# A hybrid diffusion step on one core: attention's exponentials added ahead of their sums, and GpSimd's passes given to other engines

## Chip, core and metric

The kernel runs on one core of a Trainium2 chip. The core has TensorE (PE, matmuls into PSUM), VectorE (DVE), ScalarE (ACT), GpSimd (POOL) and SyncE (SP, which issues nearly all transfers). The metric is the device time of one execution in microseconds (us).

## What is computed

Two layers work on 1152 tokens of 1024 values: 1024 latent tokens and 128 prompt tokens. Each layer normalises and modulates x, projects it once into columns for three groups of heads, and projects their joined output back. Cut to what matters (the prompt attends to itself alone, the latent tokens to 128 cached keys as well):

```python
def trunk_layer(x, cvec, l, P, ctx=None):
    shift, scale, gate = adaln(cvec, P['w_mod'][l], P['b_mod'][l])
    u = layer_norm(x) * (1.0 + scale) + shift
    r, k, v, g, cq, ckv, kr, gm, xl, gl = split_in(u @ P['w_in'][l])
    ...
    y_rw, S_fin = rwkv_branch(u, r, k, v, g, S0, l, P)            # a scan over tokens, both ways
    y_mla = block_attention(qn, qr, kn, kr_all, vv) * jax.nn.silu(gm)
    y_lru, h_fin = lru_branch(xl, gl, h0, l, P)
    out = jnp.concatenate([y_rw, y_mla, y_lru], axis=-1) @ P['w_out'][l]
    return layer_norm(ALPHA * x + gate * out, P['ln_g'][l], P['ln_b'][l]), ...

def one_block(args):                                              # of block_attention
    s = (jnp.einsum('bqhd,bkhd->bhqk', qn_b, kn) + jnp.einsum('bqhr,bkr->bhqk', qr_b, kr)) * SOFTMAX_SCALE
    p = jax.nn.softmax(s, axis=-1)
    return jnp.einsum('bhqk,bkhd->bqhd', p, v)
```

## The kernel before

All matrices are float32. A product of full precision is made from a rounded high part and a low part that is the difference (`mm3`: three products); the "splits" of the text make these parts, the high one by a copy that rounds (DVE or ACT), the low one by a subtraction.

A layer runs in four stages. (1) Tokens, nine tiles of 128 in a fixed order: `load_x`, `norm_x` (statistics, POOL's power for the root, normalisation), `norm_u` (transposes on PE, shift and scale on ACT), `make_u` (high and low part), a matmul of 288 columns for v and the rope key, and the rotation of that key by six small DVE passes, a transpose and a DMA. (2) Features, groups of columns over all tokens, with the conv, gates and scans of the LRU (`lru_piece`) and the queries between them; the modulation of what comes later is computed here in pieces (`adaln_piece`, a generator with two halves: matmul and copy, then a small matmul that reads the copy). (3) Slots, 48 in a layer: 8 heads times 2 halves of the queries are 16 units of attention, and each takes 3 slots of 3 blocks of 128 keys. (4) The output projection with the last LayerNorm, tile by tile; in layer 0 the first two tiles of layer 1 are normalised in it.

The slots are written out by hand. Each has six blocks (A0, G, A1, B, C, S), filled through `at(slot, block, f)`; in a slot, the engines take the instructions in that order, as `line` keeps it. The slot loop (L1335 on) runs A0, the scores and exponentials of three blocks of keys, G, A1, B, the values, C, the sums and S. Between the attention lie the maxima of the queries to come (`max_q`, `max_last`, DVE's reduce over 1024 columns of the one PSUM buffer "b"), the scan (`win_*`: products for a tile of tokens; `inv_*`: the inverse of 64x64 blocks, by 15 pairs of POOL instructions on growing shapes; `chain_*`: the scan itself, PE with DVE copies in blocks C and B), and the group norm and gates of the outputs. `vtt`, `vts` and `vstt` are DVE's tensor-tensor, tensor-scalar and scalar-tensor-tensor forms, `gtt` is POOL's tensor-tensor, `act` and `sca_` are ACT. In the profile most of them bear the line of a helper (L116; matmuls L121); those of POOL bear their own. The sums over keys are those of the slot:

```python
for j, pe in u["pe"]:                   # three blocks of 128 keys x 512 queries
    for qt in range(4):
        mm(u["sum"][32 * qt:32 * qt + 32, 0:128], lhsT=two[:, 0:32], rhs=pe[:, 128 * qt:128 * qt + 128], ...)
```

A float32 matmul is issued as two PE instructions. Outside the slots a planner of the framework orders the work. The kernel's start loads x of two tiles, then the modulation's weights of layer 0 in eight pieces (`adaln_all`), then the first weights of the tokens.

## Time and profile before

| | us |
|---|---|
| median of 3 runs (1920.42 to 1930.34) | 1920.56 |
| the profiled execution, its whole time | 1929.06 |
| its span, first to last instruction | 1927.3 |
| PE busy | 1802.6 (94%) |
| DVE busy | 1177.3 (61%) |
| ACT busy | 944.1 (49%) |
| POOL busy | 588.9 (31%) |

The mean granted clock of PE is 0.969 of full speed. The rows below are of four kinds. A row of busy times has the stretch in us from the start of the span, its length, then the busy time (and number of instructions) of PE, PE's weight loads, DVE, ACT and POOL, the granted clock, the share of time in which the DMA engines were busy, and GB/s. A row of a timeline has the start, the duration, engine, line, operation, the names out<-in, the shapes, and how many are joined in the row; in brackets the idle time before it and who ended that. A row of groups has the busy time of all, the mean in ns of one, the idle time before and its releasers. A row of waits has the sum, the number and the longest.

### The profile page before, as it was taken

The page shows a single profiled execution, that of the slowest core. Times are in us where ns is not written, and L with a number is a line of the kernel's source. Part 1 is how long each engine was busy: PE and PEld are TensorE (multiplying, and loading weights), DVE is VectorE, ACT ScalarE, POOL GpSimd, SP SyncE. Part 2 cuts the span into 40 slices and gives each one's busy share as a digit, 9 for nine tenths or more (in the row PEclk, how much of TensorE's full clock was granted, in tenths as well). Part 3 has the DMA queues.
Part 4 walks back from the last instruction along what each step waited for, and adds up shares of the span by engine and source line. Part 5 has one row for each costly group of instructions (what it writes and reads, how often), then busy time and mean ns, then how long its engine had stood idle before and what let it go on. Part 6 is the DMA issues. An engine that isn't in the chain of part 4 may idle for free.

```text
span 1927.3 us, 47961 instructions
## 1 busy us (share of the span) xinstructions
PE 1802.6 (94%) x18782; PEld 1510.9 (78%) x18782; DVE 1177.3 (61%) x2454; ACT 944.1 (49%) x2159; POOL 588.9 (31%) x1055
## 2 busy tenths in 40 slices
PE   6899999889999999998978999999889999999897
PEld 4798888877787777766867999998767777777586
DVE  6744444784555655765778353548755566666576
ACT  2542556773444544554225335678544454555421
POOL 1411002032344434322645110111235344342253
PEclk8999999989999999999988999999899999999899
DMA  8335444674344444436443252435633433333642
GB/s 303 100 98 166 122 131 134 213 233 126 76 113 109 112 109 108 120 104 200 153 141 115 85 185 78 133 103 193 202 93 77 99 91 86 84 86 86 214 131 88
DMA packets 329091, 250.39 MB, mean 130 GB/s; under 512 B 105304, under 2 KB 268704, under 8 KB 327840
## 3 DMA queue, kind: packets, MB, share of 16 engines
q1 hardware_dynamic: 328864, 247.32, 43.7%
q8 instruction: 148, 2.42, 0.5%
q14 instruction: 79, 0.65, 0.1%
HBM read 168.55 MB, written 78.64 MB: 128 GB/s over the span
## 4 chain that ended last, share of the span: by engine, by line
PE 56%; DVE 7%; DMA 6%; ACT 4%; issue 3%; POOL 1%; SPq 1%; DVEq 0%; POOLq 0%; ACTq 0%
PE ps_a L121 36%; PE ps_pv L121 7%; PE ps_b L121 5%; PE ps_cx L121 4%; PE ps_rw L121 4%; DVE rw L116 2%; DVE sm L116 2%; DVE ls L116 1%; DVE t L116 1%; ACT rw L116 1%; ACT t L116 1%; DMA mxb<-inv_d 1%; ACT pe L116 1%; POOL rw L1416 1%; DMA kp<-in_wout_dram 1%
## 5 line engine op out<-in xcount | busy, mean ns | idle before, releaser
L121 PE MATMUL ps_a<-t,t 128*128 128x384 f32 (+4 forms) x6096 | 710.5, 295 | 20.7 <-DVE t L116 7.5
L121 PEld LDWEIGHTS ps_a<-t,t 128*128 128x128 f32 (+1 forms) x6096 | 652.9, 167 | 50.0 <-ACT pe L116 12.3
L116 DVE TENSOR_REDUCE sm<-ps_b 128x1 f32<-128x1024 f32 (+1 forms) x164 | 179.8, 1096 | 124.6 <-PE ps_b L121 124.2
L116 ACT ACTIVATE pe<-ps_a 128x512 f32<-128x512 f32 (+1 forms) x296 | 168.6, 576 | 175.0 <-PE ps_a L121 163.2
L121 PE MATMUL ps_a<-q,t 128*128 128x512 f32 x864 | 221.3, 401 | 4.9 <-DVE ep L116 4.9
L121 PEld LDWEIGHTS ps_a<-q,t 128*128 128x128 f32 x864 | 161.2, 190 | 47.9 <-issue 7.5
L121 PE MATMUL ps_a<-t,q 128*128 128x512 f32 (+1 forms) x544 | 163.5, 384 | 0.0
L116 DVE TENSOR_TENSOR t<-kp,t 128x512 fp32r<-128x512 f32 (+2 forms) x128 | 87.4, 710 | 106.5 <-ACT t L116 106.4
L121 PE MATMUL ps_pv<-pe,t 128*64 128x256 f32 x928 | 124.3, 389 | 0.0
L121 PEld LDWEIGHTS ps_a<-t,q 128*128 128x128 f32 x544 | 101.0, 190 | 22.2
L121 PE MATMUL ps_a<-t,kp 128*128 128x512 f32 (+1 forms) x304 | 118.0, 388 | 0.0
L116 ACT CAST t<-kp 128x512 fp32r<-128x512 f32 (+2 forms) x128 | 72.1, 600 | 84.8 <-DMA kp<-in_wft_dram 39.6
L121 PE MATMUL ps_b<-t,q 96*128 96x512 f32 (+1 forms) x384 | 107.3, 374 | 2.6 <-ACT t L116 1.5
L524 POOL TENSOR_TENSOR rw<-rw 128x512 f32<-128x512 f32 (+1 forms) x24 | 19.9, 831 | 262.6 <-ACT rw L116 174.5
L861 POOL TENSOR_TENSOR t<-t 64x15 f32<-64x15 f32 (+2 forms) x270 | 71.9, 266 | 58.9 <-DVE t L116 22.0
L121 PEld LDWEIGHTS ps_pv<-pe,t 128*64 128x64 f32 x928 | 59.7, 137 | 34.2 <-issue 7.7
L116 ACT ACTIVATE rw<-rw,sm 128x512 f32<-128x512 f32 x35 | 26.7, 809 | 119.6 <-DVE sm L116 115.9
L157 POOL TENSOR_TENSOR sm<-sm,nhalf 128x1 f32<-128x1 f32 (+1 forms) x54 | 34.1, 632 | 162.4 <-DVE sm L116 159.7
L121 PEld LDWEIGHTS ps_b<-t,q 96*128 96x128 f32 x384 | 61.9, 190 | 25.3 <-issue 9.9
L862 POOL TENSOR_TENSOR t<-t 64x15 f32<-64x15 f32 (+2 forms) x270 | 73.0, 270 | 20.4
L116 DVE TENSOR_TENSOR t<-ps_a,t 128x512 f32<-128x512 f32 (+2 forms) x106 | 65.5, 625 | 17.4 <-ACT t L116 9.7
L121 PE MATMUL ps_rw<-pe,two 128*32 128x128 f32 x1888 | 75.5, 277 | 0.0
(262 smaller groups left out, 3154.9 us busy)
## 6 DMA issues: line engine op xcount, KB each, us to landing
kp<-in_wft_dram SPq DMA_DIRECT2D x64, 256.0 KB
...
t<-v_d SPq DMA_DIRECT2D x144, 64.0 KB
```

The lines of the kernel that those rows point to most:

```text
L116: return lambda *a, **k: in_line(getattr(self.eng, op)(*a, **k))
L121: return in_line(nc.tensor.matmul(*a, **k))
L157: gtt(out, t[:, :n], nhalf.to_broadcast([128, n]), op=POW)
L524: gtt(q_, a_, a_, op=MUL)
L861: gtt(tv, U_[0:64, 0:t, t:t + 1].to_broadcast([64, t, n]), X[0:64, t:t + 1, t:16].to_broadcast([64, t, n]), op=MUL)
L862: gtt(X[0:64, 0:t, t:16], X[0:64, 0:t, t:16], tv, op=ADD)
L1416: (vtt if end and j else gtt)(z, z, lgb[:, 0, js], op=MUL)
```

## The change

The diff does six things.

1. Sums: DVE adds the exponentials of a slot's three blocks (`add_exps`, after A1 and after C), and `sums` takes one block instead of three, one slot later and ahead of the values. The reciprocal (`invert`) and what follows it move one slot back.
2. POOL's tensor passes become DVE's: the low split of u and of q, the sum of the rope queries, the square in the LRU, the gates, the masks of the window, the blocks of the inverse, two passes of the group norm, the low split and a product in the output projection. POOL keeps the powers, memsets and the pairs of `inv_blocks16`, which are now taken one by one through sixteen blocks of the order.
3. `norm_x` normalises on ACT; of four modulations in `norm_u` DVE makes one; the last LayerNorm is two DVE passes a half instead of ACT, POOL and DVE.
4. The rope keys stay in one tile, and `rope_tiles` rotates all of them in the loop of stage 2 that makes the queries' and keys' rows, at its third tile.
5. Start: the vectors of both layers are loaded and worked on first; the modulation's pieces come in the order 0, 4, 1, 5, then the first token weights, then 2, 6, 3, 7; the 1 of 1 + scale is added with the bias.
6. In the features the second half of a modulation piece runs with the next step (`ada_steps`) instead of at once.

Its changed lines, with the heads of functions (lines of context are left out; "..." stands between the hunks):

```diff
     def ada_mod(ada, pm, m0, nj):
-        vtt(modT[:, m0:m0 + nj, :], pm[:, 0:2 * nj].rearrange("p (j s) -> p j s", s=2),
-            vec[:, V_BM + m0:V_BM + m0 + nj, None].to_broadcast([128, nj, 2]), op=ADD)
-    def ada_one(modT):
-        vec_.tensor_scalar(modT[:, 8:16, :], modT[:, 8:16, :], 1.0, None, op0=ADD)
+        vstt(modT[:, m0:m0 + nj, :], pm[:, 0:2 * nj].rearrange("p (j s) -> p j s", s=2), 1.0 if m0 >= 8 else 0.0,
+             vec[:, V_BM + m0:V_BM + m0 + nj, None].to_broadcast([128, nj, 2]), ADD, ADD)
     def ada_mm(ps, cw, wm):
...
-    def adaln_all(l, ada):
-        for n in range(8):
+    def adaln_all(l, ada, ns):
+        for n in ns:
-            pm = P("rw")
+            pm = P("pv")
-        ada_one(ada[1])
     def adaln_piece(l, ada, n, half_):
...
-            if (n, half_) == (7, 1):
-                ada_one(ada[1])
...
+        vstt(mv[:, 3:4], mv[:, 0:1], -1.0, mv[:, 2:3], MUL, MUL)
-            vts(xt, xt, mv[:, 0:1], mv[:, 2:3], op0=SUB, op1=MUL)
+            act(xt, xt, AF.Identity, bias=mv[:, 3:4], scale=mv[:, 2:3])
     def norm_u(l, modT, i, tag="rw2"):
...
-                act(uf[:, j, :], ps[:, 128 * j:128 * j + 128], AF.Identity, bias=modT[:, k, s:s + 1], scale=modT[:, 8 + k, s:s + 1])
+                pj, sc, sh = ps[:, 128 * j:128 * j + 128], modT[:, 8 + k, s:s + 1], modT[:, k, s:s + 1]
+                if j < 3:
+                    act(uf[:, j, :], pj, AF.Identity, bias=sh, scale=sc)
+                else:
+                    vts(uf[:, j, :], pj, sc, sh, op0=MUL, op1=ADD)
-    ada = adaln_begin(0)
-    adaln_all(0, ada)
-    w1 = first_weights(0)
-    for l in range(layers):
-        last = l == L - 1
-        vec, modT, gate_row = ada
-        def vc(base, i=0, n=1):
-            return vec[:, base + i:base + i + n]
+    def layer_vectors(l, vec):
...
+        return hv, kah, omk, m4sp
+    adas = [adaln_begin(l_) for l_ in range(layers)]
+    lvec = [layer_vectors(l_, adas[l_][0]) for l_ in range(layers)]
+    ada = adas[0]
+    adaln_all(0, ada, (0, 4, 1, 5))
+    w1 = first_weights(0)
+    adaln_all(0, ada, (2, 6, 3, 7))
+    for l in range(layers):
+        last = l == L - 1
+        vec, modT, gate_row = ada
+        def vc(base, i=0, n=1):
+            return vec[:, base + i:base + i + n]
+        hv, kah, omk, m4sp = lvec[l]
...
-                gtt(Ub[b][1][:, 4 * hf:4 * hf + 4, cs], uf, hi, op=SUB)
+                vtt(Ub[b][1][:, 4 * hf:4 * hf + 4, cs], uf, hi, op=SUB)
...
+        kr = W("ls", [128, NTILE, 16, 2])
...
-            vt = W("pe", [128, 288])
-            sca_.copy(vt, ps[:, :288])
-            dma(v_d[ts_].rearrange("t e f c -> t (e f c)"), vt[:, 0:256])
-            kr = vt[:, 256:288]
+            vt = W("pe", [128, 256])
+            sca_.copy(vt, ps[:, :256])
+            dma(v_d[ts_].rearrange("t e f c -> t (e f c)"), vt)
+            vec_.tensor_copy(kr[:, i].rearrange("p j e -> p (j e)"), ps[:, 256:288])
-                dma(kr_out[l], kr)
-            kx = kr.rearrange("p (j e) -> p j e", e=2)
-            tr = W("ls", [128, 6, 16])
-            ko = W("ep", [128, 2, 16])
-            vtt(tr[:, 0], kx[:, :, 0], kcos[:, i], op=MUL)
-            vtt(tr[:, 1], kx[:, :, 1], ksin[:, i], op=MUL)
-            vtt(tr[:, 2], kx[:, :, 0], ksin[:, i], op=MUL)
-            vtt(tr[:, 3], kx[:, :, 1], kcos[:, i], op=MUL)
-            vtt(ko[:, 0], tr[:, 0], tr[:, 1], op=SUB)
-            vtt(ko[:, 1], tr[:, 2], tr[:, 3], op=ADD)
-            pt = P("pv" if n_ % 2 else "b")
-            transpose(pt[:32, :128], ko.rearrange("p a b -> p (a b)"), ident)
-            kT = W("ls", [32, 128])
-            sca_.copy(kT, pt[:32, :128])
-            dma(krT_d[:, 128 + 128 * i:256 + 128 * i], kT)
+                dma(kr_out[l], kr[:, i].rearrange("p j e -> p (j e)"))
+        def rope_tiles():
+            tr, ko = W("pe", [128, 3, NTILE, 16]), W("ls", [128, NTILE, 2, 16])
+            vtt(tr[:, 0], kr[:, :, :, 0], kcos, op=MUL)
+            vtt(tr[:, 1], kr[:, :, :, 1], ksin, op=MUL)
+            vtt(ko[:, :, 0], tr[:, 0], tr[:, 1], op=SUB)
+            vtt(tr[:, 2], kr[:, :, :, 0], ksin, op=MUL)
+            vtt(tr[:, 0], kr[:, :, :, 1], kcos, op=MUL)
+            vtt(ko[:, :, 1], tr[:, 2], tr[:, 0], op=ADD)
+            pt = P("pv")
+            for b in range(3):
+                transpose(pt[:96, 128 * b:128 * b + 128], ko[:, 3 * b:3 * b + 3].rearrange("p i a j -> p (i a j)"), ident)
+            kT = W("pe", [96, 3, 128])
+            sca_.copy(kT, pt[:96, :384].rearrange("p (b t) -> p b t", b=3))
+            for q_ in range(3):
+                dma(krT_d[:, 128:128 + NT].rearrange("c (b i t) -> i c b t", b=3, i=3)[q_], kT[32 * q_:32 * q_ + 32])
...
-                gtt(t1, t1, t2, op=ADD)
+                vtt(t1, t1, t2, op=ADD)
...
+            if i == 2:
+                rope_tiles()
...
-                gtt(q_, a_, a_, op=MUL)
+                vtt(q_, a_, a_, op=MUL)
...
-            ada = adaln_begin(l + 1)
+            ada = adas[l + 1]
+        ada_open = []
+        def ada_steps():
+            for piece in ada_open:
+                next(piece, None)
+            ada_open.clear()
...
+            ada_steps()
-                for _ in adaln_piece(*todo):
-                    pass
+                ada_open.append(adaln_piece(*todo))
+                next(ada_open[-1])
...
-                    gtt(v_, v_, mask[:, d, None, 64:128].to_broadcast([128, 4, 64]), op=MUL)
+                    vtt(v_, v_, mask[:, d, None, 64:128].to_broadcast([128, 4, 64]), op=MUL)
         def win_transposes(i):
...
+                yield
...
-                gtt(Of[:, d].rearrange("p a (b c) -> p a b c", b=4), abz[:, d].rearrange("p f s (b c) -> p (f s) b c", b=4),
+                vtt(Of[:, d].rearrange("p a (b c) -> p a b c", b=4), abz[:, d].rearrange("p f s (b c) -> p (f s) b c", b=4),
         def inv_blocks():
-            for o, t_, ttt in ((1, BdT, vtt), (0, Bd, gtt)):
-                ttt(t_.rearrange("p d a (b j) -> p (d a) b j", b=4), Bdc[:, o, :, None, :].to_broadcast([128, 8, 4, 16]),
+            for o, t_ in ((1, BdT), (0, Bd)):
+                vtt(t_.rearrange("p d a (b j) -> p (d a) b j", b=4), Bdc[:, o, :, None, :].to_broadcast([128, 8, 4, 16]),
         def inv_product(i, n):
...
-            gtt(y4, y4, lnx[:, 1, None].to_broadcast([128, n, 2, 64]), op=ADD)
+            vtt(y4, y4, lnx[:, 1, None].to_broadcast([128, n, 2, 64]), op=ADD)
-            gtt(vt8, vt8, bon[:, c0:c0 + n].rearrange("p c f -> p (c f)")[:, :, None].to_broadcast([128, g, 64]), op=MUL)
+            vtt(vt8, vt8, bon[:, c0:c0 + n].rearrange("p c f -> p (c f)")[:, :, None].to_broadcast([128, g, 64]), op=MUL)
...
-            gtt(qo[0:96], ql, qh[0:96], op=SUB)
+        def split_low(u):
+            qo = u["qo"]
+            vtt(qo[0:96], qo[0:96].bitcast(F32), u["qh"][0:96], op=SUB)
         def max_q(u, qt):
...
-        def sums(u):
+        def sums(u, pe, first, last_):
-            for j, pe in u["pe"]:
-                if j == 0:
-                    u["sum"] = P("rw")
-                for qt in range(4):
-                    mm(u["sum"][32 * qt:32 * qt + 32, 0:128], lhsT=two[:, 0:32], rhs=pe[:, 128 * qt:128 * qt + 128],
-                       start=j == 0, stop=j == end)
-                if j == end:
-                    u["rl"] = W("ls", [128, 128])
-                    vec_.reciprocal(u["rl"], u["sum"][:, 0:128])
-            u["pe"] = []
+            if first == 0:
+                u["sum"] = P("rw")
+            for qt in range(4):
+                mm(u["sum"][32 * qt:32 * qt + 32, 0:128], lhsT=two[:, 0:32], rhs=pe[:, 128 * qt:128 * qt + 128],
+                   start=first == 0, stop=last_ == end)
+        def invert(u):
+            u["rl"] = w2[:, u["i"] % 2, 0:128]
+            vec_.reciprocal(u["rl"], u["sum"][:, 0:128])
+        def add_exps(u, n):
+            if n == 1:
+                u["acc"] = W("ls", [128, 512])
+                vtt(u["acc"], u["pe"][0][1], u["pe"][1][1], op=ADD)
+            else:
+                vtt(u["acc"], u["acc"], u["pe"][2][1], op=ADD)
         def load_gate(u):
...
         def gate(u):
-            gtt(gm, gm, u["o"], op=MUL)
+            vtt(gm, gm, u["o"], op=MUL)
...
+            at(s0 - 5, "C", split_low, u)
...
-                at(s0 + 3, "C", finish, u)
-                at(s0 + 4, "G", gate, u)
+                at(s0 + 4, "C", finish, u)
+                at(s0 + 5, "G", gate, u)
...
-            at(c - 8, "C", inv_blocks16)
+            sub_ = inv_blocks16()
+            for k_ in range(16):
+                k6 = 6 * (c - 8) + 4 + 3 * k_ // 4
+                at(k6 // 6, ("A0", "G", "A1", "B", "C", "S")[k6 % 6], next, sub_, None)
...
         def prompt(u):
-            sums(u)
+            sums(u, u["pe"][0][1], 0, 0)
+            invert(u)
+            u["pe"] = []
...
+            split_low(u)
+        ada_steps()
...
+        behind = None
...
+            add_exps(u, 1)
+            if behind:
+                sums(*behind)
-            sums(u)
+            add_exps(u, 2)
+            if slot % 3 == 0 and behind:
+                invert(behind[0])
+            behind = u, u.pop("acc"), u["pe"][0][0], u["pe"][-1][0]
+            u["pe"] = []
+        sums(*behind)
+        invert(us[-1])
...
-                (vtt if early else gtt)(l_, yr, h_, op=SUB)
+                vtt(l_, yr, h_, op=SUB)
...
-            vstt(mv[:, 3:4], mv[:, 0:1], -1.0, mv[:, 2:3], MUL, MUL)
-                if j or not end:
-                    act(z, z, AF.Identity, bias=mv[:, 3:4], scale=mv[:, 2:3])
-                else:
-                    vts(z, z, mv[:, 0:1], mv[:, 2:3], op0=SUB, op1=MUL)
-                (vtt if end and j else gtt)(z, z, lgb[:, 0, js], op=MUL)
-                vtt(z, z, lgb[:, 1, js], op=ADD)
+                vstt(z, z, mv[:, 0:1], lgb[:, 0, js], SUB, MUL)
+                vstt(z, z, mv[:, 2:3], lgb[:, 1, js], MUL, ADD)
```

## Rows read from the trace of the kernel before

**Rows 1.** Busy time by stage (stretch, length, engines, clock, DMA share, GB/s).

```profile
0.00:39.00 39.00, 21.60 (x172) 12.50 (x173) 20.60 (x93) 7.39 (x18) 1.31 (x6) 0.83 0.93 324
39.00:101.00 62.00, 52.45 (x340) 48.51 (x340) 49.59 (x139) 34.40 (x101) 28.23 (x28) 0.94 0.40 125
101.00:480.00 379.00, 352.03 (x2291) 320.24 (x2290) 201.40 (x437) 202.36 (x476) 60.49 (x94) 0.95 0.49 152
480.00:884.00 404.00, 396.02 (x6467) 305.39 (x6466) 251.20 (x520) 204.44 (x452) 151.12 (x359) 0.99 0.43 112
1003.00:1060.00 57.00, 43.08 (x276) 39.54 (x275) 48.41 (x123) 32.10 (x88) 29.78 (x28) 0.88 0.42 133
...
1419.00:1804.00 385.00, 379.51 (x6157) 291.22 (x6155) 239.75 (x480) 200.40 (x445) 149.04 (x354) 1.00 0.37 94
```

**Rows 2.** Timeline of PE in a slot of layer 1: sums over keys.

```profile
1646.14 0.43 PE L121 MATMUL ps_rw<-pe,two 128*32 128x128 f32 x8
1646.38 0.40 PE L121 MATMUL ps_rw<-mxb,two 128*32 128x128 f32 x8
1646.60 0.40 PE L121 MATMUL ps_rw<-pe,two 128*32 128x128 f32 x8
```

**Rows 3.** Timeline of DVE in a slot: three passes of 128x512.

```profile
873.45 1.90 DVE L116 TENSOR_TENSOR t<-kp,t 128x512 fp32r<-128x512 f32 x3 [0.73 <-ACT t L116]
```

**Rows 4.** Groups of DVE by shape, slots of layer 1.

```profile
L116 DVE TENSOR_REDUCE sm<-ps_b 128x1 f32<-128x1024 f32 x59 | 71.3, 1208 | 49.1 <-PE ps_b L121 49.0
...
L116 DVE TENSOR_TENSOR t<-ps_a,t 128x512 f32<-128x512 f32 x27 | 18.6, 690 | 2.8 <-PE ps_a L121 2.1 <-POOL t L861 0.3
...
L116 DVE TENSOR_TENSOR st<-ps_cx,st 128x256 f32<-128x256 f32 x18 | 7.6, 425 | 24.5 <-PE ps_cx L121 23.9 <-issue 0.6
```

**Rows 5.** Groups of POOL by shape, slots of layer 1.

```profile
L1072 POOL TENSOR_TENSOR q<-q,q 96x512 fp32r<-96x512 f32 x14 | 17.8, 1270 | 24.8 <-ACT q L116 21.8 <-PE ps_a L121 3.0
L1169 POOL TENSOR_TENSOR ep<-ep,ep 128x256 f32<-128x256 f32 x17 | 12.5, 735 | 35.1 <-DVE ep L116 26.6 <-ACT t L116 5.1 <-DMA q<-qr_d 2.2
...
L862 POOL TENSOR_TENSOR t<-t 64x63 f32<-64x63 f32 x16 | 4.8, 301 | 1.3
```

**Rows 6.** Busy time in three slots: first, one of 94, last.

```profile
479.78:487.32 7.54, 7.54 (x67) 5.00 (x66) 4.91 (x8) 3.21 (x6) 2.55 (x6) 1.00 0.47 122
...
781.80:789.60 7.80, 7.80 (x134) 6.31 (x132) 6.78 (x20) 3.38 (x7) 3.03 (x3) 1.00 0.43 115
1799.51:1804.01 4.50, 4.50 (x45) 2.92 (x45) 1.38 (x5) 3.27 (x8) 1.47 (x2) 1.00 0.98 335
```

**Rows 7.** Waits of PE in the features of layer 0.

```profile
PE ps_a L121 <- DVE ep L116: 15.3, 7, 3.6
```

**Rows 8.** Timeline of PE: one of these seven waits.

```profile
368.97 0.58 PE L121 MATMUL ps_a<-kc,ep 128*128 128x2 f32 x2 [3.65 <-DVE ep L116]
```

**Rows 9.** Busy time in three token tiles of layer 0.

```profile
67.85:84.75 16.90, 13.09 (x93) 11.71 (x94) 15.56 (x42) 9.47 (x27) 9.41 (x9) 1.00 0.30 93
```

**Rows 10.** Timeline of DVE in these tiles: rope, its sum, normalisation of x.

```profile
75.02 1.14 DVE L116 TENSOR_TENSOR ls<-pe,kc 128x16 f32<-128x16 f32 x4
...
76.20 0.20 DVE L116 TENSOR_TENSOR ep<-ls 128x16 f32<-128x16 f32 x2
...
77.24 1.96 DVE L116 TENSOR_SCALAR rw<-rw,sm 128x512 f32<-128x512 f32 x2 [0.44 <-POOL sm L157]
```

**Rows 11.** Timeline of POOL in the token tiles: a low split.

```profile
74.58 1.29 POOL L341 TENSOR_TENSOR t<-rw,t 128x512 fp32r<-128x512 f32 x1 [1.75 <-DVE t L116]
```

**Rows 12.** The page's groups: ACT normalising in the output projection.

```profile
L116 ACT ACTIVATE rw<-rw,sm 128x512 f32<-128x512 f32 x35 | 26.7, 809 | 119.6 <-DVE sm L116 115.9
```

**Rows 13.** Timeline of PE at the start of layer 1's tokens.

```profile
1011.00 0.85 PE L121 MATMUL ps_a<-t,t 128*128 128x288 f32 x2 [4.43 <-DVE t L116]
```

**Rows 14.** Timeline of DVE there.

```profile
1009.92 0.69 DVE L116 BATCH_NORM_STATS2 sm<-rw 128x6 f32<-128x512 f32 x1 [3.54 <-DMA rw<-x_d]
1010.53 0.41 DVE L116 CAST t<-rw 128x512 fp32r<-128x512 f32 x1
```

**Rows 15.** Timeline of PE between the layers.

```profile
975.23 1.12 PE L124 MATMUL ps_rw<-kc,ls 128*128 128x128 f32 x4 [5.31 <-DVE ls L116]
```

**Rows 16.** Timeline of DVE between the layers: the same pass beside POOL and alone.

```profile
943.47 1.79 DVE L116 TENSOR_TENSOR rw<-rw,t 128x512 f32<-128x512 f32 x1
...
978.82 0.68 DVE L116 TENSOR_TENSOR rw<-rw,t 128x512 f32<-128x512 f32 x1
```

**Rows 17.** Busy time in the output projection of layer 0.

```profile
889.00:969.90 80.90, 79.97 (x345) 63.85 (x345) 54.44 (x73) 19.48 (x32) 40.48 (x31) 0.98 0.49 154
```

**Rows 18.** Timeline of PE: the first token matmul.

```profile
39.06 0.83 PE L121 MATMUL ps_a<-t,t 128*128 128x288 f32 x2
```

## The prediction

> **What bounds the kernel now.** I read the busy time of each engine by stage first. The stages are start-up, token projections, features, slots of layer 0, and then the token projections and slots of layer 1 [rows 1]. In the slots TensorE (PE) is busy 396.0 of 404 us and 379.5 of 385 us, so PE is the bound there, and only less PE work can shorten them, as long as VectorE (DVE), now at 251 and 240 us, stays below. In the token stages PE is busy 52.5 of 62 us and 43.1 of 57 us, while DVE has 49.6 and 48.4 us: there the wait on DVE matters. In the features PE has 352 of 379 us: 27 us of gaps. In the first 39 us the DMA share is 0.93 and PE waits for weights. After that I read, stage by stage, the waits of PE and what released them.
>
> **Part 1, sums over the keys.** A slot's sum now is 24 PE instructions of 128 columns, 8 for each block of 128 keys; where the trace shows the blocks apart, they start 0.24 and 0.22 us after each other [rows 2]: 28 ns an instruction in the shorter, since the four groups of 32 output columns run side by side. Adding the three exponentials first leaves one block, so 16 instructions go: 16 x 0.028 = 0.45 us a slot, and over 2 x 48 slots 43 us. That is the ceiling of this part. The Trainium skill, TensorE: Matmul & The Clock Gate, section "Wait — 56ns, not 53.3ns?", gives 56 ns from one 128-column matmul to the next. By it the 1,536 instructions would be worth an estimated 86 us; the row shows half of that, and the measurement decides.
>
> The price is two DVE adds of 128x512 a slot. Three DVE passes of that size took 1.90 us [rows 3], so two are some 1.3 us (0.69 each alone [rows 4]). They stand in the DVE queue, which runs in order: add 1 after block A1 has issued, add 2 after block C. Behind them wait the copies of the scan chain (block B, C) and the max reduce of the next A0, whose PSUM buffer is the only one of its tag. DVE now waits for PE ahead of the 59 max reduces of a layer for 49.1 us, 0.83 us each [rows 4], so there is slack in front of just these.
>
> **Part 2, GpSimd (POOL) to DVE in the slots.** Seven groups of POOL instructions move: two of 512 columns (x14 and x9, 1.26 to 1.27 us each) and five of 256 (66 in all, 0.61 to 0.76 us each); one of either stands in [rows 5]. DVE does such passes in 0.69 and 0.425 us [rows 4], so a layer moves 23 x 0.69 + 66 x 0.425 = 44 us to DVE. POOL was not the bound, so what it loses brings nothing by itself. What stays on POOL is the inverse of the blocks, in pieces of up to 0.30 us [rows 5], now strewn over 16 blocks of a slot's order.
>
> DVE in the slots is then 240 + 48 x 1.3 + 44 = 346 us (layer 1) and 251 + 62 + 44 = 357 us (layer 0), beside PE at 379.5 - 22 = 358 and 396 - 22 = 374. So the averages still fit, by 12 and 17 us, but not every slot does. I went through the 47 windows between the starts of neighbouring slots in each layer, took 0.45 us off PE, added 1.3 us and the POOL instructions of that slot to DVE, and kept the larger. The first and the last of layer 0 and layer 1 [rows 6] fit (7.09 against 4.91 + 1.3 + 0.86 = 7.06 us; 4.05 against 3.54); the one at 781.80 doesn't: PE 7.35, DVE 6.78 + 1.3 + 1.12 = 9.2 us. DVE is the longer one in 13 and 17 of 47 slots. The sum of the larger falls from 400.3 to 392.8 and from 385.0 to 380.0: **-13 us**. Nothing may be carried from slot to slot in this count; with all slots evened out it would be -43. The bad end is that nothing is hidden (below). I take -13, since PE's max and scan chain wait on the DVE queue within a slot.
>
> **Part 3, the second half of a modulation piece one step later.** In the features of layer 0 each piece's matmul waits at once for a copy by DVE: 7 waits, 15.3 us, the longest 3.6 [rows 7]; one stands in [rows 8]. When the second half runs in the next step, the copy has long been made. Ends: 0 (PE waits for another thing at the same place) and -18 (shorter waits under the list too). I take **-14**.
>
> **Part 4, token stages.** Three tiles take 16.90 us, 5.63 each, with DVE busy 15.56 and PE 13.09 [rows 9]: DVE bound, 5.19 us of DVE a tile. The rope leaves (1.14 + 0.20 us) and so does the normalisation of x (1.96 us for two halves) [rows 10]. Added are two low splits, which cost POOL 1.29 us each [rows 11] and DVE 0.69, two modulations of 128x128 of some 0.3, a copy of 0.2 and a small one of 0.15. That is 5.19 - 3.30 + 1.38 + 0.6 + 0.35 = 4.2 us. ScalarE (ACT) gets 2 x 0.81 us [rows 12] less two modulations of 0.38: 3.16 + 0.86 = 4.0. PE has 4.36. So PE is next, and a tile takes some 4.9 with what is left of the waits: 9 x 0.7 = **-6** in layer 0. The rope as a whole comes back once, six passes of 144 columns and three transposes, in a loop where DVE has room (features: 201 of 379 us). In layer 1 the waits of PE sum to 57 - 43 = 14 us, one of 4.43 us for the DVE cast of a tile [rows 13]; but DVE itself has then waited 3.54 us for the DMA of x, which the layer before has just written [rows 14], and the change leaves that. Of the other 10 us I take **-6**. Ends for both together: 0 and -20, the whole of the waits that can go.
>
> **Part 5, between the layers.** PE waits 5.31 us for the normalised x of the next layer's first tile [rows 15]. DVE is slowed there: a pass of 128x512 takes 1.79 us, and 0.68 a little later [rows 16]; POOL works on the same lines in the first case. On ACT and without POOL's multiplications I take **-3** (ends 0, -5). The output projection before it is bound by PE, 79.97 of 80.9 us, with DVE at 54.4 [rows 17]; the two splits and two more passes that come to DVE there are 4 x 0.69 = 2.8 us a tile, some 21 us for the 7.5 tiles of this stretch, so 75 of 81: nothing on the path. If that cover were gone, the splits alone would be 9 x 2 x 0.69 = 12 us a layer.
>
> **Part 6, start-up.** The first token matmul starts at 39.06 [rows 18]. The bytes ahead of it stay nearly the same, but with pieces 0, 4, 1, 5 first the first half of a tile can be modulated before the rest has come, and the vector chain, now on DVE between tokens, moves ahead into the time in which DVE waits for DMA. SP's queue is passed by the vectors of layer 1, a small load. I take **-5**; ends +3 (the vectors of layer 1 delay the first piece) and -10.
>
> **The sum.** -13 - 14 - 6 - 6 - 3 - 5 = -47 us. The profiled execution took 1929.06 us, 8.5 above the median of 1920.56; so 1882 for such an execution, and 1874 against the median.
>
> **The rivals.** *A, DVE holds the slots:* DVE at 95 to 97% of PE's time, in order, stalls PE as often as the sums give back. In the token stage DVE reached 92% of the time [rows 9], and in the slots it would need 346 of the 358 us that PE has left in layer 1. For it: 30 of 94 slots too long. Then parts 1 and 2 bring 0: 1887. *C, all of it comes:* slack before the reduces soaks up the adds [rows 4], PE stays the bound: -43 for -13, and 1844. *D, it doesn't do what it says:* the step later and the new order of LN leave PE waiting for the next thing, so parts 3 to 6 bring nothing and the slots alone -13: 1908. *B, slower:* both adds come to lie on PE's path, since the reduce of the next A0 and the chain's copies stand behind them in one queue: +1.3 - 0.45 = +0.87 a slot (1.3 is the two passes), 96 times, +83, and the rest -34: 1874 + 13 + 83 = 1970. It decides from the point where more than 0.45 us a slot of the adds is not hidden; against it speak the 0.83 us for which DVE waits before a reduce [rows 4]. For it: an add may meet an inverse piece on POOL, and then cost up to 0.30 us more [rows 5], as the slow pass of [rows 16] cost 1.1 us more beside a longer one. The Trainium skill, SBUF — State Buffer, section "Who interferes with whom", says that DVE and GpSimd share one pair of ports and that the loser fully blocks, which is the case for an add with both operands in SBUF. [rows 16] fits that, and it speaks against the adds; but the same change takes most of POOL's work away.
>
> **How the numbers follow.** Forecast (1874) 0.50; C 0.17; A 0.19; D 0.06; B 0.08. About 0.5% (1911 to 1930) is what a measurement of this kernel can tell from no change. Faster: the forecast, C, A and most of D, 0.88; same 0.04; slower 0.08. The range leaves out B and D: from 1838 (C with start-up at -10, 1839) to 1905 (A with features at -4 and tokens at -4 instead of -14 and -12): 0.86.
>
> **What would show it.** Sum blocks of 8 instructions at about 0.25 us; slots of 385 and 375 us with DVE at 90% or more; no wait of over 1 us on ep in the features; token tiles of 4.9 us with PE the busiest; the wait at 975 near 2 us. Waits of PE's max scores on the reduces, or of the chain on DVE copies, above 1 us in most slots would show A or B. Wrong it would be if DVE passes were slower by contention than 0.69 us, or if the planner put the moved passes at other places.

## The result: slower by 1.4%

The changed kernel takes 1955.63 us in the median of 4 runs (1953.85 to 1959.77), beside 1925.45 us for the kernel before in the same comparison: a ratio of 1.0138 with a 95% interval of 1.0109 to 1.0166. The forecast was 1874 (1838 to 1905). The profiled execution took 1954.45 us, its span is 1952.7.

Busy time by stage in the kernel after, to be held against [rows 1] (stretch, length, PE, weight loads, DVE, ACT, POOL, granted clock, DMA share, GB/s):

```profile
39.00:101.00 62.00, 54.64 (x344) 50.99 (x341) 42.84 (x112) 36.68 (x88) 4.78 (x10) 0.89 0.37 115
...
475.00:889.00 414.00, 385.69 (x5705) 279.75 (x5705) 332.23 (x702) 203.12 (x450) 91.17 (x271) 1.00 0.41 109
1007.00:1064.00 57.00, 43.41 (x272) 38.61 (x271) 41.68 (x107) 34.22 (x77) 4.86 (x10) 0.91 0.40 123
...
1421.80:1824.44 402.64, 374.08 (x5398) 270.57 (x5396) 322.95 (x659) 200.61 (x447) 89.70 (x266) 0.98 0.35 89
```

The slots, which should have lost 13 us, have become the stage that grew: 414 us instead of 404, and 403 instead of 385. PE has fewer instructions there (5398 instead of 6157 in layer 1) and nearly the same busy time (374 instead of 380 us), but it now stands idle for some 29 us instead of 5; DVE went from 240 to 323 us (forecast: 346). The token stages show the work leaving DVE (49.6 to 42.8 us, 48.4 to 41.7), and no time won.

The table gives, for all kernels of this study, the length of each stage in the profiled execution, worked out from the starts of the first matmuls of neighbouring stages (first token matmul, last token matmul, first score of the first slot, first score of the last slot, and so on), and the ratio to the kernel before. Each ratio is to the kernel before in the same comparison, where its median was 1925 to 1932 us, so differences between experiments go by the ratios. The stages are those of one execution each, and the executions of a kernel lie apart (E4: 1909.8, the one in the table, to 1919.6): a stage that differs by a few us, with no wait behind it, shows nothing.

| kernel | ratio (95%) | start | tokens 0 | features 0 | slots 0 | to layer 1 | tokens 1 | features 1 | slots 1 | rest |
|---|---|---|---|---|---|---|---|---|---|---|
| before | 1 | 39.1 | 55.9 | 384.8 | 400.3 | 123.0 | 60.5 | 355.4 | 385.0 | 119.7 |
| after | 1.0138 (1.0109-1.0166) | 39.0 | 55.4 | 380.7 | 410.0 | 122.1 | 60.4 | 354.2 | 402.6 | 125.2 |
| E1 three sums | 0.9972 (0.9950-0.9993) | 38.3 | 55.6 | 380.0 | 399.1 | 116.4 | 61.0 | 357.4 | 387.7 | 121.3 |
| E2 adds alone | 1.0223 (1.0189-1.0257) | 38.8 | 55.7 | 387.1 | 412.1 | 122.1 | 61.9 | 355.0 | 412.9 | 122.7 |
| E4 no adds | 0.9928 (0.9910-0.9946) | 39.1 | 55.6 | 376.8 | 390.0 | 121.5 | 61.0 | 356.2 | 380.7 | 124.3 |
| E5 adds late | 0.9990 (0.9968-1.0012) | 37.7 | 56.6 | 377.8 | 405.8 | 119.7 | 53.1 | 354.0 | 388.7 | 123.4 |
| E6 adds on POOL | 1.0127 (1.0102-1.0152) | 39.3 | 55.3 | 380.8 | 415.8 | 116.6 | 53.0 | 359.8 | 404.1 | 127.0 |
| E7 pieces at once | 0.9966 (0.9945-0.9987) | 37.1 | 56.1 | 390.1 | 401.7 | 115.8 | 53.2 | 357.8 | 389.6 | 120.3 |
| E8 norm on DVE | 0.9991 (0.9975-1.0007) | 37.6 | 60.1 | 382.3 | 398.9 | 116.1 | 60.4 | 356.0 | 392.0 | 119.8 |
| E9 POOL kept | 0.9951 (0.9934-0.9968) | 38.7 | 55.2 | 386.6 | 400.5 | 118.5 | 54.1 | 362.1 | 386.9 | 121.1 |
| E10 adds in light slots | 0.9892 (0.9857-0.9928) | 39.4 | 53.7 | 378.2 | 392.3 | 123.5 | 54.4 | 355.2 | 385.5 | 123.5 |
| E11 end in three | 1.0093 (1.0066-1.0121) | 38.8 | 56.0 | 382.5 | 416.1 | 116.0 | 53.1 | 356.3 | 409.9 | 119.4 |
| E12 start order | 0.9972 (0.9951-0.9993) | 34.8 | 56.9 | 380.8 | 403.2 | 117.6 | 63.6 | 357.5 | 389.2 | 119.4 |
| E13 one block | 0.9798 (0.9765-0.9830) | 39.5 | 54.6 | 377.7 | 388.0 | 116.9 | 53.4 | 356.1 | 377.6 | 118.9 |

**Where a slot loses.** The waits of PE in the slots of layer 1 (sum, number, longest), after:

```profile
PE ps_b L121 <- DVE sm L116: 14.8, 20, 2.3
PE ps_a L121 <- DVE ys L116: 8.9, 7, 2.4
PE ps_rw L121 <- DVE w L116: 2.5, 1, 2.5
```

Before, the same view had two of the three:

```profile
PE ps_b L121 <- DVE sm L116: 3.1, 1, 3.1
...
PE ps_a L121 <- DVE ys L116: 0.2, 1, 0.2
```

They are the max reduce (sm), the inverse's product (ys) and the reciprocal (w). A slot and the one that follows show it, as rows of busy time:

```profile
1488.33:1496.87 8.54, 8.18 (x131) 6.27 (x129) 6.23 (x10) 4.20 (x9) 4.79 (x15) 1.00 0.38 93
1496.87:1507.82 10.95, 9.11 (x156) 6.59 (x154) 10.05 (x22) 3.65 (x8) 0.42 (x2) 1.00 0.29 61
```

The second lasts 10.95 us though neither engine is that long in it: PE 9.11, DVE 10.05. So the two are not merely of unequal length, they wait for each other. Its DVE timeline, and PE's two waits:

```profile
1497.31 0.68 DVE L116 TENSOR_TENSOR ls<-ls,mxb 128x512 f32<-128x512 f32 x1
1497.91 0.95 DVE L116 RECIPROCAL w<-ps_rw 128x128 f32<-128x128 f32 x1
1498.78 1.16 DVE L116 TENSOR_REDUCE sm<-ps_b 128x1 f32<-128x1024 f32 x1
...
1502.15 0.68 DVE L116 TENSOR_TENSOR ls<-pe,pe 128x512 f32<-128x512 f32 x1
1502.76 0.42 DVE L116 TENSOR_TENSOR ys<-ps_a,ys 128x256 f32<-128x256 f32 x1
```

```profile
1499.99 0.66 PE L121 MATMUL ps_b<-t,q 96*128 96x128 f32 x4 [0.86 <-DVE sm L116]
...
1503.23 1.09 PE L121 MATMUL ps_a<-t,t 64*64 64x128 f32 x28 [0.98 <-DVE ys L116]
```

Ahead of the reduce at 1498.78 DVE makes add 2 of the slot before (1497.31) and the reciprocal (1497.91), 1.5 us in all, while the scores that it should reduce lie in the only buffer "b"; PE waits 0.86 us for it. At 1502.15 add 1 stands ahead of the copy ys, and PE waits 0.98 us. In the groups of DVE (layer 1) the slack that should have hidden the adds is gone. First the reduces and some of the adds in the changed kernel:

```profile
L116 DVE TENSOR_REDUCE sm<-ps_b 128x1 f32<-128x1024 f32 x59 | 71.1, 1205 | 13.9 <-PE ps_b L121 13.8
L116 DVE TENSOR_TENSOR ls<-ls,pe 128x512 f32<-128x512 f32 x38 | 26.2, 689 | 0.4
```

Then the same reduces in E1 (three sums, no adds), E13 (the sum of one block, in its own slot) and E4 (the sum of one block a slot later, no adds):

```profile
L116 DVE TENSOR_REDUCE sm<-ps_b 128x1 f32<-128x1024 f32 x59 | 71.3, 1208 | 42.8 <-PE ps_b L121 42.7
```

```profile
L116 DVE TENSOR_REDUCE sm<-ps_b 128x1 f32<-128x1024 f32 x59 | 71.2, 1207 | 30.8 <-PE ps_b L121 30.4
```

```profile
L116 DVE TENSOR_REDUCE sm<-ps_b 128x1 f32<-128x1024 f32 x59 | 71.3, 1208 | 25.6 <-PE ps_b L121 25.0
```

DVE's wait for PE before the 59 reduces was 49.0 us [rows 4] and is 13.8. The adds (0.69 us each, as priced) took only the last 11 of these 35 us. Of the others, 6 went with the other parts of the change (to 42.7), 12 with the two blocks of sums (to 30.4) and 5 with the later sum (to 25.0), ahead of any add: part of the slack was PE's time for the sums that part 1 removes.

The waits have a second price in layer 1. In its slots the granted clock of PE was at the lower of its two levels, 1.2 instead of 2.4 GHz, in four stretches of 3.4 to 6.8 us, 17 us in all (3.4 before and in E4), each beside or just behind a wait of PE for DVE of 1.35 to 2.47 us. A busy row and two rows of PE from one of them, then the same nine matmuls at the full clock:

```profile
1803.50:1810.00 6.50, 6.19 (x23) 3.63 (x25) 5.33 (x22) 3.60 (x9) 0.89 (x1) 0.50 0.55 168
```

```profile
1803.60 0.59 PE L121 MATMUL ps_b<-kc,sm 128*4 128x128 f32 x2 [2.30 <-DVE sm L116]
1804.40 4.21 PE L121 MATMUL ps_a<-q,t 128*128 128x512 f32 x9 [0.21 <-DVE ep L116]
```

```profile
1496.87 2.27 PE L121 MATMUL ps_a<-q,t 128*128 128x512 f32 x9
```

They take 4.21 us instead of 2.27. An estimate from these numbers: half of the 14 us more, some 7 of the 17.6 us that layer 1 lost. In layer 0 the clock was at the lower level for 3.4 us (before 6.8), and explains nothing there.

### The profile page after: what moved, and what is told of

Same layout as the page of the kernel before. It is cut to its first block, busy times and chain, and to the rows that moved or that the text cites. A ratio compares the mean times of both kernels' runs of the same rounds, so it can differ in the third digit from the quotient of the medians.

```text
span 1952.7 us, 44576 instructions
## 1 busy us (share of the span) xinstructions
PE 1783.8 (91%) x17234; PEld 1466.5 (75%) x17234; DVE 1347.7 (69%) x2902; ACT 929.4 (48%) x2108; POOL 277.6 (14%) x718
## 5 line engine op out<-in xcount | busy, mean ns | idle before, releaser
L121 PE MATMUL ps_a<-t,t 128*128 128x384 f32 (+4 forms) x6096 | 716.2, 296 | 54.6 <-DVE t L116 15.4
L116 ACT ACTIVATE pe<-ps_a 128x512 f32<-128x512 f32 (+1 forms) x296 | 168.0, 576 | 127.7 <-PE ps_a L121 116.1
L116 DVE TENSOR_TENSOR t<-kp,t 128x512 fp32r<-128x512 f32 (+2 forms) x128 | 81.8, 666 | 84.3 <-ACT t L116 74.6
L882 POOL TENSOR_TENSOR t<-t 64x15 f32<-64x15 f32 (+2 forms) x270 | 85.8, 318 | 318.9 <-DVE t L116 299.2
L157 POOL TENSOR_TENSOR sm<-sm,nhalf 128x1 f32<-128x1 f32 (+1 forms) x54 | 39.7, 735 | 476.5 <-DVE sm L116 461.8
L883 POOL TENSOR_TENSOR t<-t 64x15 f32<-64x15 f32 (+2 forms) x270 | 84.1, 312 | 20.8
L116 ACT CAST q<-pe 128x512 fp32r<-128x512 f32 x32 | 19.9, 621 | 120.1 <-PE ps_a L121 96.5
L121 PEld LDWEIGHTS ps_cx<-t,t 128*64 128x64 f32 (+1 forms) x1752 | 63.4, 138 | 15.2 <-issue 7.3
L121 PE MATMUL ps_cx<-t,t 128*64 128x64 f32 (+1 forms) x1752 | 71.2, 226 | 0.9 <-ACT t L116 0.8
```

The lines of the kernel that those rows point to most:

```text
L116: return lambda *a, **k: in_line(getattr(self.eng, op)(*a, **k))
L121: return in_line(nc.tensor.matmul(*a, **k))
L157: gtt(out, t[:, :n], nhalf.to_broadcast([128, n]), op=POW)
L882: gtt(tv, U_[0:64, 0:t, t:t + 1].to_broadcast([64, t, n]), X[0:64, t:t + 1, t:16].to_broadcast([64, t, n]), op=MUL)
L883: gtt(X[0:64, 0:t, t:16], X[0:64, 0:t, t:16], tv, op=ADD)
```

## Experiments

Theory 1: the adds and the reciprocal cost by their place in DVE's queue, ahead of the reduce and the inverse's copies. Theory 2: DVE is too full, with 44 us a layer from POOL, wherever the adds stand.

**E1, three sums.** Part 1 undone in the changed kernel.

```diff
-            add_exps(u, 1)
...
-            if behind:
-                sums(*behind)
...
-            add_exps(u, 2)
+            sums(u)
...
-                at(s0 + 4, "C", finish, u)
+                at(s0 + 3, "C", finish, u)
```

> The changed kernel with part 1 alone undone: three blocks of sums on PE in the same slot, no adds, finish and gate a slot earlier, as before. Theory 1 (the two adds and the reciprocal stand ahead of the max reduce and of the inverse's copies in DVE's queue, and PE waits behind them): the 27 us that the slots grew go away, so 1915 to 1930. Theory 2 (the passes that came from POOL fill DVE in the heavy slots; the adds matter little): the waits stay and PE gets 2 x 19 us of sums back, 1985 to 1995.

1923.64 us, ratio 0.9972: the slots are back at 399.1 and 387.7. Part 1 as built costs 1.66%, 32 us; all the other parts together are worth 0.3%, some 5 us. Theory 2 expected 1985 or more.

**E2, adds alone.** Part 1 alone in the kernel before.

> The kernel before with part 1 alone: adds, sums of one block a slot later. POOL keeps its passes. Theory 1: the waits come back for the same reason, slots longer by some 20 us, 1935 to 1950. Theory 2: PE's 2 x 19 us come out whole, 1885 to 1890. Both at work (the adds need slack that only the passes from POOL take): between, about 1905.

1971.40 us, ratio 1.0223: above both theories. The place in the queue is the same, so are the waits on the reduce. Waits of PE, and the longest wait of SP's DMA queue, layer 1:

```profile
PE ps_b L121 <- DVE sm L116: 15.1, 19, 2.7
PE ps_a L121 <- DMA t<-zr_d: 13.4, 5, 6.2
```

```profile
SPq L1180 <- POOL ep L1176: 43.7, 8, 14.6
```

On top there are 13.4 us for the window's load. In this kernel the gate, now a slot later, is POOL's and stands behind the burst of inverse pieces; its store is issued by SP, whose queue stands for 43.7 us and with it the loads behind it (before, SP's waits for this store come to 14.4 us). That moving the gate to DVE and strewing the inverse keep part 1 from costing more is argued from this trace; no run has them one by one.

**E4, no adds.** The changed kernel without the adds.

```diff
-            add_exps(u, 1)
...
-            add_exps(u, 2)
...
-            behind = u, u.pop("acc"), u["pe"][0][0], u["pe"][-1][0]
+            behind = u, u["pe"][-1][1], u["pe"][0][0], u["pe"][-1][0]
```

> The changed kernel without the two adds of a slot: the sums read the exponentials of the slot's last block alone, so the sums over keys leave out two blocks of three, and one is added to the sum ahead of the reciprocal. PE's work is that of the changed kernel. It measures what the adds cost by themselves. Theory 1: 1885 to 1900 (the forecast without any price for the adds, some 13 us under 1887). Theory 2: 1945 to 1956, since the passes from POOL still hold the slots.

1915.37 us, ratio 0.9928. The adds by themselves cost 2.1%, 40 us (in the table the slots: 20.0 and 21.9), or 0.42 us of the 1.3 us of a slot's two adds: the larger part was hidden, and it was not enough. But without them the time is 1915, not the 1885 to 1900 of theory 1: a second thing is wrong with the forecast (E13).

**E5, adds late.** The same adds, behind block B and behind the next slot's A0, and the reciprocal behind the second of them.

```diff
             run(slot, "A0")
+            add_last()
...
-            add_exps(u, 1)
             run(slot, "B")
...
             values(u)
+            add_exps(u, 1, u["pe"])
             run(slot, "C")
-            add_exps(u, 2)
```

> The changed kernel with the same adds in other places of the order: add 1 behind block B (so behind the copies of the inverse) and add 2 with the reciprocal behind block A0 of the next slot (so behind the max reduce). Same work on every engine. Theory 1: the waits of PE on the reduce and on the inverse shrink by more than half, 1915 to 1930. Theory 2: DVE is as full as before, 1950 to 1960.

1927.24 us, ratio 0.9990: 1.5% or 28 us faster than the change with the same work on each engine. Waits of PE, layer 1:

```profile
PE ps_a L121 <- DVE ys L116: 8.3, 7, 2.1
PE ps_b L121 <- DVE sm L116: 4.1, 2, 2.9
```

The reduce's waits fell from 14.8 to 4.1 us; those on ys stayed (8.9, now 8.3). Some 7 us of the 28 are the token stage of layer 1 (53.1 instead of 60.4), which the edit does not touch (below); 18 are the slots. Without these 7 us the time would be some 1934, above the range of theory 1, so its number was met by luck. The places are worth 18 of the 42 us that the adds cost in the slots; at the late places they still cost 24 more than in E4, and the slots stay 8 us above those of E1. Whether that is the places, still ahead of ys or the reciprocal, or DVE's load, no run separates.

**E6, adds on POOL.**

```diff
-                vtt(u["acc"], u["pe"][0][1], u["pe"][1][1], op=ADD)
+                gtt(u["acc"], u["pe"][0][1], u["pe"][1][1], op=ADD)
...
-                vtt(u["acc"], u["acc"], u["pe"][2][1], op=ADD)
+                gtt(u["acc"], u["acc"], u["pe"][2][1], op=ADD)
```

> The changed kernel with the two adds of a slot on POOL instead of DVE, at the same places of the order. DVE's queue is then that of the kernel without adds. Theory 1 (what costs is the adds' place in DVE's queue): near the kernel without adds (1915), so 1912 to 1926. Rival (two engines that both read SBUF hold each other up, as the pass of 1.79 us instead of 0.68 in the trace of before suggests): 2 x 1.27 us of POOL a slot slow DVE's two-input passes, 1940 or more.

1955.71 us, as slow as the change: the rival was right. A group of DVE and one of POOL in layer 1 of E6, and then the same group of DVE in E4, where no add runs:

```profile
L116 DVE TENSOR_TENSOR t<-abz,kc 128x256 f32<-128x256 f32 x18 | 15.7, 910 | 0.3
```

```profile
L1175 POOL TENSOR_TENSOR ls<-ls,pe 128x512 f32<-128x512 f32 x37 | 48.1, 1299 | 1.7
```

```profile
L116 DVE TENSOR_TENSOR t<-abz,kc 128x256 f32<-128x256 f32 x18 | 6.9, 422 | 0.3
```

This DVE pass with two inputs in SBUF takes 910 instead of 422 ns beside POOL's adds. DVE's busy time in the slots is 304.9 and 299.4 us, 25 more a layer than in E4. In layer 1 PE's waits on the reduce fell to 8.7 us, those on ys rose to 13.6; for a sum of POOL itself it waits once, 0.4 us. Taking work off DVE's queue gave nothing, since POOL slowed what stayed in it.

**E7, pieces at once** (on E1), part 3 undone.

```diff
-            ada_steps()
             for todo in ada_todo[:ka]:
-                ada_open.append(adaln_piece(*todo))
-                next(ada_open[-1])
+                for _ in adaln_piece(*todo):
+                    pass
```

> The changed kernel with three blocks of sums (1924) and, on top of it, part 3 undone: both halves of a modulation piece at once. Theory (the seven waits did not go, they moved to the next feature's PSUM buffer, which ACT frees late): within 4 us of 1924, and the features of layer 0 within 4 us of its 380. Rival (part 3 brought its 14 us and another part lost them): 1934 to 1940.

1923.10 us, ratio 0.9966: no difference in time, as the theory had it, but its number for the features was missed: 390.1 us, 10 more than in E1. Waits of PE in the features of layer 0, first E7, then E1:

```profile
PE ps_a L121 <- DVE ep L116: 20.0, 10, 7.1
PE ps_a L121 <- ACT pe L116: 5.2, 2, 4.5
```

```profile
PE ps_a L121 <- ACT pe L116: 11.5, 4, 6.6
PE ps_b L121 <- ACT t L116: 4.7, 1, 4.7
PE ps_a L121 <- DVE ep L116: 4.7, 1, 4.7
```

Part 3 takes 15 us of waits on ep away and others come for them, on ACT above all. The 10 us are too much for what it keeps: E7's one execution had the lower clock for 41 us of this stage, E1's for 31. Over all kernels the features of layer 0 take 376.8 to 386.6 us with part 3 (eleven kernels, mean 380.4) and 384.8, 387.1 and 390.1 without it (before, E2, E7), some 7 us. That does not appear in E7's time because its token stage of layer 1 is 7.8 us shorter, for a reason that has nothing to do with the edit (below).

**E8, norm on DVE** (on E1).

```diff
-            act(xt, xt, AF.Identity, bias=mv[:, 3:4], scale=mv[:, 2:3])
+            vts(xt, xt, mv[:, 0:1], mv[:, 2:3], op0=SUB, op1=MUL)
```

> The changed kernel with three blocks of sums (1924) and x normalised by DVE again. Theory (ACT's normalisation stands behind casts that wait for weights from DMA, so that it gives back what DVE saves): within 4 us of 1924, token stages within 2 us of 55.6 and 61. Rival (the token stages gained on DVE and lost on the clock alone): 6 to 12 us slower, 1930 to 1936, DVE bound again at 5.4 to 5.6 us a tile.

1927.34 us, ratio 0.9991; the intervals of E1 and E8 overlap. The token stage of layer 0 is 4.5 us longer (60.1), that of layer 1 the same (60.4 beside 61.0): the theory met the time, and missed the stage of layer 0 by more than its 2 us. In layer 0 ACT's normalisation is worth 4.5 us.

**E9, POOL kept** (on E1): the seven groups of the slots on POOL again.

```diff
-            vtt(gm, gm, u["o"], op=MUL)
+            gtt(gm, gm, u["o"], op=MUL)
```

(and the same in the six others)

> The changed kernel with three blocks of sums (1924) and the seven groups of passes in the slots on POOL again; the other parts stay. It separates part 2 in the slots from the rest. Theory 1 (DVE has room for 44 us a layer as long as no adds stand in its queue): within 4 us of 1924. Rival (the moved passes by themselves cost the slots several us): 1912 to 1918.

1921.54 us, ratio 0.9951. The slots are 400.5 and 386.9 us beside E1's 399.1 and 387.7. DVE's busy time there is 246.3 and 241.3 us, in E1 278.4 and 271.6: the moved passes are 31 us a layer, not 44, and cost nothing as long as no adds stand in its queue. Theory 2 falls as far as it blames these passes alone; what they cost beside the adds no run shows.

**E13, one block** (on E1): two blocks of three left out of the sums, in their own slot.

```diff
             for j, pe in u["pe"]:
-                if j == 0:
+                if j % 3 != f_:
+                    continue
+                if j == f_:
```

> The changed kernel with part 1 undone (1924), and two of a slot's three blocks left out of the sums over keys (one is added ahead of the reciprocal); nothing is moved to a later slot. It measures what the 16 PE instructions a slot are worth by themselves. Theory 1 (the slots are PE's as long as DVE's queue is free): the ceiling of 38 to 43 us, 1881 to 1886. Rival (the sums filled time in which PE would wait for the reduces, the exponentials and the scan's copies, and half of their time turns into waits): 1900 to 1910.

1896.26 us, ratio 0.9798, 33 us under E1 by the ratios (their intervals leave some 7 us to either side). It does not have E1's longer token stage of layer 1 (53.4 instead of 61.0), so the sums are worth about 26, of which 21 in the slots (388.0 and 377.6 beside 399.1 and 387.7): PE is busy 32 us less there and waits 11 us more. Between the two expectations, nearer to the rival. From E13 to E4, which moves the sum a slot later and still has no adds, the time goes up by 1.3%, 25 us: 7.6 the token stage again, 5 the slots, and 10 the ends of the two layers' slots (the stretch to layer 1 from 116.9 to 121.5, the rest from 118.9 to 124.3). In that stretch the kernel before (123.0) has the wait of [rows 15], which is gone in all kernels with part 5; those of them that sum in the unit's own slot take 115.8 to 118.5 us, but for E10. The waits of PE in it, in E1, and the longest one in the changed kernel:

```profile
PE ps_a L121 <- DVE ls L116: 4.9, 1, 4.9
PE ps_a L121 <- DVE ep L116: 2.7, 1, 2.7
```

```profile
PE ps_rw L121 <- DVE ls L116: 7.9, 1, 7.9
...
```

E6 (later sum, 116.6) and E10 (own slot at the end, 123.5) don't fit, and why stays open.

**E11, end in three.** The changed kernel, the last unit without adds.

```diff
-            add_exps(u, 2)
+            if slot < end_:
+                add_exps(u, 2)
...
+                for j, pe in u["pe"]:
+                    sums(u, pe, j, j)
```

> The changed kernel (1956) with the last unit of either layer summed in three blocks in its own slots, without adds. Theory (the sum a slot later lengthens the end of the slots: waits of 7.8 and 3.7 us after the last scores, where the kernel before waits 4 us once): 5 us a layer back, 1944 to 1948. Rival (those waits lie beside the weights' splits, which hold DVE anyway): within 3 us of 1956.

1952.07 us, ratio 1.0093, between the two expectations; its interval overlaps that of the change, and 7 us of the gain are the token stage of layer 1 (53.1). The stretch to layer 1 is at 116.0 us and the rest behind the slots of layer 1 at 119.4, 6 us less than after in both; the slots grew by 6 and 7 us, some of it in the last unit itself, and took it back. So the drain is real, and this edit is no cure. What E11 removes are these two waits of PE behind the last scores of the changed kernel's layer 1, where the kernel before waits once, for 4.05 us:

```profile
1837.99 0.66 PE L121 MATMUL ps_rw<-ls,two 128*32 128x128 f32 x8 [7.83 <-DVE ls L116]
1842.36 0.70 PE L121 MATMUL ps_a<-w,two 32*64 32x128 f32 x8 [3.71 <-DVE w L116]
```

**E12, start order** (on E1): the pieces in order, then the first weights.

```diff
-    adaln_all(0, ada, (0, 4, 1, 5))
+    adaln_all(0, ada, range(8))
     w1 = first_weights(0)
-    adaln_all(0, ada, (2, 6, 3, 7))
```

> The changed kernel with part 1 undone (1924), and the modulation's eight pieces in their old order ahead of the first weights. Theory (part 6 brings nothing, since all eight pieces are needed for the first tile's end and DMA is full): within 4 us of 1924. Rival (it saves the 5 us of the forecast): 1929 or more.

1927.09 us, ratio 0.9972, that of E1. The first token matmul even comes 3.5 us earlier with the old order (34.8), and the tokens then take 1.3 longer: the part is worth nothing.

**E10, adds in light slots.** The late places of E5, in 25 slots of a layer; E1's trace has DVE free for 2.0 us or more in each of them, and in some that were not chosen (slots 5 and 41: 3.9 and more). Three sums in the others, the last units among them, and the reciprocal right behind its sums.

```diff
+            if slot in light:
+                add_exps(u, 1, u["pe"])
             run(slot, "C")
-            add_exps(u, 2)
+            if slot in light:
+                whole = u, u["pe"]
...
+            else:
+                for j, pe in u["pe"]:
+                    sums(u, pe, j, j)
```

> The changed kernel with adds in 25 of a layer's 48 slots, those in which the trace of the kernel with three blocks shows DVE free for 1.8 us or more, and with the adds behind block B and behind the next slot's A0; the other slots sum three blocks in their own slot, the last units too. Theory 1 (an add that finds slack and stands behind the reduce costs nothing): the gain of these slots, half of what the 16 instructions are worth, under the 1924 of the kernel without adds: 1905 to 1916. Theory 2 (adds cost what they save wherever they stand): 1922 to 1930.

1910.65 us, ratio 0.9892: faster than both kernels. The slots are 392.3 and 385.5 us, 9 under E1 together; 6.6 more are the token stage of layer 1, and without these the time would be some 1917, just above the range of theory 1. In DVE's groups the reduce has kept half of its slack (27.2 us of waiting for PE) beside the adds that remain:

```profile
L116 DVE TENSOR_REDUCE sm<-ps_b 128x1 f32<-128x1024 f32 x59 | 71.8, 1217 | 27.5 <-PE ps_b L121 27.2
```

## Why the prediction was wrong, step by step

**The slots: forecast -13, measured +27** (+9.7 and +17.6). This term carries the error. Three steps of it failed, and some 7 us of layer 1's loss are the clock behind the waits (the estimate above), which no step had.

- *"The sum of the larger."* In each slot I took the longer of PE and DVE, as if the two ran freely beside each other, and called that bound careful because nothing is carried from slot to slot. It is not a bound: within a slot PE waits for DVE twice (reduce, ys), and DVE for PE, in the order of one queue. The slot above lasts 10.95 us with 9.11 and 10.05. The right question was which DVE result PE waits for next, and what the change puts ahead of it.
- *The rival B was this mechanism, at a chance of 0.08.* Its point was right: it decides from 0.45 us a slot that is not hidden, and E4 measures 0.42 for the adds, to which the later sum adds its own. I argued against it with the mean of DVE's wait before a reduce, 0.83 us. With the sums gone and moved it is 0.42 us (E4: 25.0 us for 59 reduces) ahead of any add; and the adds and the reciprocal that come ahead of it are up to 1.5 us, and meet the slots unevenly. The mean of a slack says nothing about the slots that have none. I had the loads slot by slot and did not use them there.
- *The cost of "one slot later".* I read the moves of sum, finish and gate as free. They lengthen the drain behind the last slot, by 4.6 us in layer 0 and 5.4 in layer 1 (E13 against E4), with the last reciprocal behind the weights' splits in DVE's queue; E6 and E10 leave a doubt about the size.

The ceiling of part 1 was nearly right as time of PE: from the start of each of their matmuls to that of the next, waits left out, the sums went from 36 to 17 us in layer 1, 19 where 21.6 were reckoned. As a gain for the kernel it is about 26 of 43 us (E13), since with the sums gone PE waits 11 us more in the slots. The price of an add (0.69 us) was right.

**Part 2 in the slots: forecast none by itself; right** (E9). Its 44 us a layer and the adds' 62 were too much, 31 (E1 less E9) and some 50 (the change less E4): 346 forecast, 323 measured. So DVE's load was not underrated.

**Part 3: forecast -14, measured -4 in the changed kernel and some -7 over all kernels (E7).** The waits on ep went as forecast and others took their place. One of them, with ACT at that time:

```profile
316.81 1.65 PE L121 MATMUL ps_a<-t,t 128*128 128x384 f32 x4 [6.48 <-ACT pe L116]
```

```profile
314.98 1.28 ACT L116 ACT_TABLE_LOAD   x1
316.27 0.49 ACT L116 ACTIVATE pe<-ps_a 128x384 f32<-128x384 f32 x1
```

PE waits 6.48 us for a PSUM buffer that ACT's copy at 316.27 frees; ahead of the copy in ACT's order stand a table load (1.28 us) and work on the LRU's gates. This is the rival D, which I gave 0.06, for this part.

**Part 4: forecast -6 and -6, measured -0.5 and -0.1.** DVE's relief was right: later tiles of layer 0 take 4.75 us (78.6 - 69.1 for two), against 4.9 forecast and 5.7 before. But two things were not on my list. First, ACT's normalisation now stands behind casts of the next weights, which wait for their DMA; in layer 0:

```profile
57.99 0.62 ACT L116 CAST t<-kp 128x512 fp32r<-128x512 f32 x1 [3.33 <-DMA kp<-in_wtk_dram]
58.51 1.51 ACT L116 ACTIVATE rw<-rw,sm 128x512 f32<-128x512 f32 x2
```

ACT waits 3.33 us for weights, and x, ready before, is normalised only then. I counted ACT's busy time (4.0 us a tile), and not its queue. Second, in layer 1 the same lines come out in one of two orders. ACT in the changed kernel, and in E13:

```profile
1025.72 1.17 ACT L116 CAST t<-kp 128x512 fp32r<-128x512 f32 x2
1026.75 1.20 ACT L116 ACTIVATE rw<-ps_cx,modT 128x128 f32<-128x128 f32 x3
1028.32 0.62 ACT L116 CAST t<-kp 128x512 fp32r<-128x512 f32 x1 [0.36 <-DMA kp<-in_wtk_dram]
1030.71 0.37 ACT L116 COPY pe<-ps_a 128x256 f32<-128x256 f32 x1 [1.78 <-PE ps_a L121]
1033.36 1.52 ACT L116 ACTIVATE rw<-rw,sm 128x512 f32<-128x512 f32 x2 [2.27 <-DVE sm L116]
```

```profile
997.07 1.17 ACT L116 ACTIVATE rw<-ps_cx,modT 128x128 f32<-128x128 f32 x3
998.11 1.54 ACT L116 ACTIVATE rw<-rw,sm 128x512 f32<-128x512 f32 x2
999.52 0.62 ACT L116 CAST t<-kp 128x512 fp32r<-128x512 f32 x1
```

In E13 the next tile's normalisation (998.11) is issued ahead of the last cast; in the changed kernel it comes behind the last cast and a copy that waits 1.78 us for PE, and then waits 2.27 us itself. ACT has E13's order in E5, E6, E7, E9, E10, E11 and E13, whose stage takes 53.0 to 54.4 us, and the other one in the change, E1, E4 and E12, with 60.4 to 63.6 (E8, which normalises on DVE: 60.4). The edits that tell these kernels apart don't touch this stage: the framework's planner orders it, and came to one or the other. In the good order part 4 does bring the 6 to 7 us of the forecast.

**Part 5: forecast -3, measured -7 without part 1; in the changed kernel part 1 hides it.** The wait of 5.31 us [rows 15] is gone, and the stretch to layer 1 is 116.4 us in E1 beside 123.0. In the changed kernel it is 122.1, since the longer drain of the later sum stands in the same stretch (a wait of 7.9 us where E1 has 4.9; the rows are at E13).

**Part 6: forecast -5, measured about 0.** The start is 39.0 beside 39.1, and E12 shows that its order is worth nothing.

**The sum.** Of the 47 us forecast E1, without part 1, has 5, and E13, with the price of part 1 left out and the good order in layer 1's tokens, 39. Outside the slots the forecast was too high, by next waits that it did not look for; what made the sign wrong was part 1 alone: 33 us of gain in E13 (7.6 of them the order in layer 1's tokens), 25 lost from E13 to E4 (the same 7.6, the slots and the drains) and 40 from E4 to the change.

On the two places of the Trainium skill: the 56 ns of the Trainium skill, TensorE: Matmul & The Clock Gate, section "Wait — 56ns, not 53.3ns?", do not show for these matmuls of 32 output columns; the traces have 19 us for some 760 instructions recorded as gone in layer 1, 25 ns each. The rule of the Trainium skill, SBUF — State Buffer, section "Who interferes with whom", that an instruction of DVE with two SBUF inputs contends with a GpSimd instruction that reads SBUF, agrees with E6 (910 against 422 ns); in the changed kernel, where the adds take 0.69 us, as priced, and this pass 422 ns, it does not explain the loss.
